# A PEER layer on one core: where the one-token blocks stand in a group, the planner's price of a look-up, skipped empty gather places, and the PSUM tag of the last group's scores

## The chip, the cores and the metric

The kernel runs on one core of a Trainium2 chip. The metric is the device time of one execution in microseconds (us). The executions shown are 1198.37, 1197.64 and 1202.17 us, with a median of 1198.37 us.

## The reference, cut to what matters

One layer of a diffusion backbone: 512 latent tokens and 256 context tokens of width 1024 go through a bidirectional mLSTM, grouped-query attention, a norm, and then PEER, a retrieval of experts. The change lies in PEER. For each block of 128 tokens the reference computes

```python
s1, i1 = lax.top_k(s[:, :, 0], 16);  s2, i2 = lax.top_k(s[:, :, 1], 16)
idx = ...                       # per token 8 heads x 16 experts out of 128 x 128
g = softmax(top_s)
act = gelu(einsum('nd,ned->ne', xt, u[idx]), approximate=False)
out = einsum('ne,ned->nd', g * act, v[idx])
```

Each token picks 128 of 16384 experts; an expert is a row `u` and a row `v` of 1024 floats, kept side by side in one table of rows of 8192 bytes. Many experts are picked by one token of the block only, others by several.

## The kernel before, in words

**Groups and blocks.** The 512 tokens are four groups (NT = 4) of 128. The distinct experts of a group are listed and worked off in 29 blocks (NBL) of 128 places, an expert in each partition. The first 12 lists (NB1) hold experts that one token picked ("one-token blocks"), the other 17 hold the rest ("dense blocks"). The reference's own routing on its inputs gives 3178, 3675, 3632 and 3680 distinct experts in the four groups, with 1405, 1625, 1568 and 1640 of them picked once. 3712 places are there, so 534, 37, 80 and 32 places stay empty. In the first group the empty ones are the lists 26, 27 and 28 (dense) and 11 (one-token) as a whole and a few places more. An empty place has the number 16384 (NEXP). The list `wi` keeps that number, which points at a row of zeros behind the weights; the list `ri` is clipped to 16383, so the expert gather of an empty place fetches the last expert's row.

**A block.** `rows` (stage r, five blocks ahead) gathers the experts' rows `uv` (128 x 8192 bytes, 1.05 MB) and the weights' rows `wr` (128 x 512 bytes) through POOL's queue, line 1122. A dense block is then transposed on PE (`turn`, L1287, copied by ACT, L1288), multiplied with the group's tokens into a PSUM bank `s` (`dense`, L1301), goes through Gelu on ACT (L1302) and is multiplied by the weights on DVE (L1303). A one-token block finds each expert's token on DVE (`token`, L1162 and L1163, four blocks ahead), gathers these tokens' rows `xg` (128 x 4096 bytes, 0.52 MB; `use`, three blocks ahead), takes the products on DVE (`dot`, L1183, one block ahead) and scales on ACT (L1184, L1200). Both end in `add`: `py += wt @ v`, L1211, in PSUM. PIPE gives the stages' lead. `seqs` says which list stands at which of a group's 29 positions; before, the one-token lists stand at positions 3, 5, 7, ... 25 in the first three groups and at 1, 3, 5, 8, 10, 13, 15, 18, 20, 22, 25, 27 in the last.

**Work for the next group.** While one group's blocks run, the next group's lists are made, as a generator that is advanced by a planner: `select` (top-16 on DVE, with scratch in the big tile `work`), then `prelude`. The first part of `prelude`, here "the table", builds the dense weights of 128 x 128 x 128 in `work`: 16 chunks of one-hot tiles A and B on DVE (L1018, L1021), matmuls on PE (L1028, L1031), and ACT copies (L1033). Then 16 pieces of `work` of 512 KB each are written to `Wd` in memory through SP's queue (`rows_out`, L1038), and the lists are looked up (`tables`, `look_up`: DVE, PE L1089, ACT L1095). `select` of the group after that uses `work` again.

**The planner.** Each step of that generator has a price: C_SEL 5 and others for `select` (56 in sum), C_A 3.5 for each of 16 chunks (56), C_L 1.5 for each of 10 look-up steps (15), C_N 1 three times: 130 in sum. After each block as many steps are emitted as 130/29 per block allow, and a piece of `Wd` per step. The frame orders each engine's instructions by this program order and by what is ready.

**PSUM.** In this part the tags are "u" with two banks, "s" with one, "p" with two (the prelude's matmuls), "pf" with one, and `py` with two.

Of the kernel before, what the change touches and what calls it, by code (L numbers as in the profile page):

```python
# [23 lines left out]
NT = L // P  # L24
# [9 lines left out]
NEXP = 16384  # L34
NBL = 29
NB1 = (12, 12, 12, 12)
# [5 lines left out]
EST = (2, 1)  # L42
HLB = 2
WTB = 5
C_SEL, C_OH, C_IIG, C_A, C_L, C_N = 5, 3, 2, 3.5, 1.5, 1
WPC = 16
GH = 4
TCH = 8
# [3 lines left out]
UVB = 7  # L52
# [8 lines left out]
PIPE = (("r", 5), ("k", 4), ("u", 3), ("d", 1), ("o", 2), ("w", 1), ("h", 1), ("a", 0))  # L61
EUV = 3
HEADS = (2, 4, 6, 8, 10, 12, 14, 16, 18, 21, 24, 27, 30, 33, 38, 40)
SPREAD = 0.7
OFF = 0.5
LAG = 2
POL = 1
DMB = 3
# [9 lines left out]
def tile_block(ctx, tc, xcT, x, cb, crow, w_mod1, w_modT, w_in, conv_w, conv_b, b_gates, mhw, qnw, knw,  # L78
# [9 lines left out]
    def bank(name, tag="mm"):  # L88
        t = ps.tile([P, 512], F32, tag=tag, name=name, bufs=depth[tag])
        return t  # L90
# [43 lines left out]
    ident, triu, tril, ones = (cst[:, i, :] for i in range(4))  # L134
# [167 lines left out]
    def g4(name):  # L302
        t = mp.tile([P, 2, 8, 4], F32, name=name)
        return t

    li, lf, e1, b, blast, a, M, amb, m, Ml, winter, enm, wr, decay = (
        g4(n) for n in ("li", "lf", "e1", "b", "blast", "a", "M", "amb", "m", "Ml", "winter", "enm", "wr", "decay"))
# [585 lines left out]
    lists = [None] * NT  # L893
# [90 lines left out]
    def send(n):  # L984

        for _ in range(min(n, len(pieces))):
            f, q = pieces.pop(0)
            f(q)
# [129 lines left out]
        lists[t] = ri, wi  # L1118
        yield

    def gather(dst, src, ids):
        nc.gpsimd.indirect_dma_start(out=dst, out_offset=None, in_=src,  # L1122
                                     in_offset=bass.IndirectOffsetOnAxis(ap=ids, axis=0))


    def order_of(n1, spread):
        def at(b):
            return (b + 0.5) / n1 * spread + (1 - spread) * OFF if b < n1 else (b - n1 + 0.6) / (NBL - n1)
        return sorted(range(NBL), key=at)

    seqs = [order_of(NB1[t], SPREAD if t < NT - 1 else 1.0) for t in range(NT)]

    def blocks(bp, eb):

        n = NBL
# [6 lines left out]
        def rows(t, i):  # L1142
            b = seqs[t][i]
            if i == 0:
                send(WPC)
                hts[t] = channels(t, bp if t % 2 else eb)
            pool, bufs = (eb, EUV) if (t * n + i) % UVB < EUV else (bp, UVB - EUV)
            w = pool.tile([P, 2 * D], F32, tag="uv", name=f"uv{t}_{b}", bufs=bufs)
            gather(w, uv, lists[t][0][:, b:b + 1])
            wr = bp.tile([P, P], F32, tag="wr", name=f"wr{t}_{b}", bufs=LOOK + 2)  # L1150
            gather(wr, Wd[t][:, :], lists[t][1][:, b:b + 1])
            live[t, i] = [w, wr]
# [13 lines left out]
        def use(t, i):  # L1166

            b = seqs[t][i]
            if b < NB1[t]:
                xg = bp.tile([P, D], F32, tag="xg", name=f"xg{t}_{b}", bufs=XGB)  # L1170
                gather(xg, h2d[:, :], live[t, i].pop())
                live[t, i].append(xg)
# [14 lines left out]
        def weights(t, i):  # L1187
            b = seqs[t][i]
            if b >= NB1[t]:
                w, wr, ut = live[t, i]  # L1190
                wt = bp.tile([P, P], F32, tag="wt", name=f"wt{t}_{b}", bufs=WTB)
                dense(t, b, ut, hts[t], wr, wt)
                live[t, i] = w, wt
# [9 lines left out]
        def add(t, i):  # L1203
# [9 lines left out]
            if i == n - 1:  # L1213
# [4 lines left out]
                else:  # L1218
                    ends.append(finish(t, bp, py, lnr))

        stages = {"r": rows, "k": token, "u": use, "d": dot, "o": operand, "w": weights, "h": scaled, "a": add}
        loads = {DEFER - LOOK: 1, AT: 2, n + AT: 3}
        for i in range(-LOOK, len(items)):
            if i + LOOK == len(items):
# [3 lines left out]
                w = bp.tile([P, 2 * D], F32, tag="uv", name="lnr", bufs=UVB - EUV)  # L1228
# [6 lines left out]
            if i in loads:  # L1235

                t = loads[i]
# [53 lines left out]
    def channels(t, pool):  # L1291

        ht = pool.tile([P, KC, P], F32, tag="ht", name=f"ht{t}")
        (nc.gpsimd if t else nc.sync).dma_start(ht, h2Td[t])
        return ht

    def dense(t, b, ut, ht, gr, wt):

        s_ = bank(f"s{t}_{b}", "s")
        for k in range(KC):  # L1300
            nc.tensor.matmul(s_[:, 0:P], ut[:, k, :], ht[:, k, :], start=k == 0, stop=k == KC - 1)  # L1301
        nc.scalar.activation(wt, s_[:, 0:P], AF.Gelu)  # L1302
        nc.vector.tensor_tensor(wt, wt, gr, op=ALU.mult)  # L1303
# [44 lines left out]
    with tc.tile_pool(name="bp", bufs=1, reuse_waits="tile") as bp:  # L1348
        n = NBL
# [22 lines left out]
    with tc.If(most > NBL):  # L1372
        with tc.tile_pool(name="fb", bufs=1) as fb:
            for t in range(NT):
# [8 lines left out]
                with tc.For_i(0, P):  # L1383

                    pm = fb.tile([P, 3, P], F16, tag="fpm", name=f"fpm{t}")
                    nc.vector.tensor_scalar(pm[:, 2], ig[:, 0], bc[:, 0:1], None, op0=ALU.is_equal)
                    for q in range(2):
                        nc.vector.tensor_tensor(pm[:, q], pm[:, 2], ig[:, 2 + q], op=ALU.mult)
                    pl = bank(f"fpl{t}", "p")
                    for c in range(P // TCH):  # L1390
                        A = fb.tile([P, P, TCH], F16, tag="fA", name=f"fA{t}_{c}", bufs=2)
                        nc.vector.tensor_tensor(A, iob, ig[:, 1, c * TCH:(c + 1) * TCH].unsqueeze(1).to_broadcast([P, P, TCH]),
                                                op=ALU.is_equal)
                        for i in range(TCH):
                            j = c * TCH + i
                            for q in range(2):
                                nc.tensor.matmul(pl[:, j:j + 1], A[:, :, i], pm[:, q, j:j + 1], start=q == 0, stop=q == 1)
                    gr = fb.tile([P, P], F32, tag="fgr", name=f"fgr{t}")
                    nc.scalar.mul(gr, pl[:, 0:P], 1.0 / GSC)
                    ri = fb.tile([P, 1], I32, tag="fri", name=f"fri{t}")  # L1400
                    nc.vector.tensor_copy(ri, bc[:, 1:2])
                    w = fb.tile([P, 2 * D], F32, tag="uv", name=f"fw{t}", bufs=2)
                    gather(w, uv, ri)
                    wt = fb.tile([P, P], F32, tag="fwt", name=f"fwt{t}")
                    dense(t, "f", turn(t, "f", fb, w), ht, gr, wt)
                    py = ps.tile([P, D], F32, tag="y", name=f"fpy{t}", bufs=1)
                    for half in range(2):
                        hs = slice(half * 512, half * 512 + 512)
                        nc.tensor.matmul(py[:, hs], wt, w[:, D + half * 512:D + half * 512 + 512], start=True, stop=True)
                    nc.vector.tensor_tensor(y, y, py, op=ALU.add)  # L1410
                    nc.vector.tensor_scalar_add(bc[:, 0:1], bc[:, 0:1], 1.0)
                    nc.vector.tensor_scalar_add(bc[:, 1:2], bc[:, 1:2], float(P))
# [81 lines left out]
```

## Time and profile before

| what | value |
|---|---|
| median of the executions | 1198.37 us |
| profiled execution, its own time | 1204.68 us |
| its span (first to last instruction) | 1202.9 us |
| granted TensorE clock, mean | 0.931 |
| PE, DVE, ACT, POOL busy | 1038.4, 826.4, 464.8, 465.7 us |
| moved by DMA | 284.15 MB, 236 GB/s over the span |

The blocks run from 612 to 1189 us of the span: the four groups' sums `py` are complete near 766, 918, 1076 and 1189 us. In what follows "DMA share" is the mean busy share of the core's 16 DMA engines, and PEclk the granted TensorE clock as a share of full speed.

### The profile page before, as it was taken

What the parts mean: (1) busy time and instruction counts of PE and PEld (TensorE: products, weight loads), DVE (VectorE), ACT (ScalarE), POOL (GpSimd) and SP (SyncE); (2) the same over time, 40 slices, a digit from 0 to 9 for tenths busy, and PEclk for the clock granted to TensorE, in tenths of its full rate; (3) what the DMA queues carried; (4) which work ended last, traced back from release to release, by engine and by line L of the source; (5) the groups of instructions that cost most, each with busy time, mean ns of one, the idle gap of its engine ahead of it and who ended that gap; (6) DMA issues with size and microseconds to landing.
All of it is one profiled execution on the core that took longest, in us unless ns stands there. A gap on an engine that the chain in (4) does not pass through costs nothing.

```text
span 1202.9 us, 19211 instructions
## 1 busy us (share of the span) xinstructions
PE 1038.4 (86%) x6784; PEld 837.7 (70%) x6784; DVE 826.4 (69%) x2698; ACT 464.8 (39%) x1132; POOL 465.7 (39%) x374
## 2 busy tenths in 40 slices
PE   6889689799989999999378987989788797897985
PEld 5688678688988888898346765668555576565663
DVE  5958999869875778377795857989379785223213
ACT  3343353465562121245433454344343353522221
POOL 3643234222023520000345542656335544355760
PEclk7899899989989999999679997999899899898998
DMA  9656450220035498512978889988997877989983
GB/s 364 226 202 217 168 177 36 74 80 15 1 102 173 159 274 252 172 39 108 384 249 305 280 299 371 330 333 286 339 401 282 301 280 285 417 318 340 377 315 115
DMA packets 109038, 284.15 MB, mean 236 GB/s; under 512 B 9316, under 2 KB 62280, under 8 KB 92936
## 3 DMA queue, kind: packets, MB, share of 16 engines
q0 software_dynamic: 28048, 157.04, 35.2%
q1 hardware_dynamic: 75864, 120.32, 29.0%
q10 hardware_dynamic: 5024, 5.51, 1.3%
q8 instruction: 55, 0.90, 0.3%
q14 instruction: 47, 0.39, 0.1%
HBM read 237.17 MB, written 45.66 MB: 235 GB/s over the span
## 4 chain that ended last, share of the span: by engine, by line
PE 38%; DVE 16%; DMA 10%; issue 8%; ACT 2%; SPq 1%; POOL 1%; another core or an unknown queue 0%; DVEq 0%; ACTq 0%; POOLq 0%
PE py L1211 8%; PE pwq L839 8%; PE s L1301 4%; DMA xg<-h2d,ti 4%; PE pW L1031 3%; PE pw L770 2%; PE put L1287 2%; PE po L542 2%; DMA Wd<-work 2%; DVE work L900 2%; DMA uv<-in_uv,ri 2%; DVE work L899 1%; DVE work L902 1%; DVE work L901 1%; PE pf L1028 1%
## 5 line engine op out<-in xcount | busy, mean ns | idle before, releaser
L1211 PE MATMUL py<-uv,wt 128*128 128x512 f32 x464 | 239.7, 636 | 14.6 <-DVE wt L1303 7.8
L1122 POOL DMA_INDIRECT uv<-in_uv,ri x116 | 119.1, 1026 | 133.4 <-PE py L1211 65.0
L1301 PEld LDWEIGHTS s<-ht,ut 128*128 128x128 f32 x1088 | 141.4, 202 | 37.1 <-ACT wt L1302 18.3
L1301 PE MATMUL s<-ht,ut 128*128 128x128 f32 x1088 | 151.5, 289 | 14.8 <-ACT wt L1302 13.9
L1122 POOL DMA_INDIRECT wr<-Wd,wi x116 | 125.6, 1083 | 69.5 <-issue 35.6
L1211 PEld LDWEIGHTS py<-uv,wt 128*128 128x128 f32 x464 | 83.1, 203 | 70.0 <-issue 53.8
L1288 ACT COPY ut<-put 128x512 f32<-128x512 f32 x136 | 75.2, 588 | 102.3 <-PE put L1287 72.1
L1031 PEld LDWEIGHTS <-A 128*128 128x128 f16 x1024 | 89.7, 146 | 20.3 <-issue 13.1
L1033 ACT ACTIVATE work<-pW 128x512 f32<-128x512 f32 x128 | 73.5, 597 | 78.2 <-PE pW L1031 66.5
L1031 PE MATMUL pW<-B,A 128*128 128x128 f16 x1024 | 95.3, 225 | 6.4 <-ACT work L1033 2.9
L1287 PEld LDWEIGHTS put<-cst,uv 128*128 128x128 f32 x544 | 68.3, 152 | 41.8 <-issue 29.9
L1122 POOL DMA_INDIRECT xg<-h2d,ti x48 | 57.9, 1206 | 94.1 <-DVE ti L1163 44.6
L839 PE MATMUL pwq<-h2T,wq 128*128 128x256 f32 x416 | 94.2, 379 | 0.0
L1287 PE MATMUL put<-cst,uv 128*128 128x128 f32 x544 | 80.3, 291 | 15.4 <-DMA uv<-in_uv,ri 13.0
L1183 DVE SCALAR_TENSOR_TENSOR xg<-xg,uv 128x1024 f32<-128x1024 f32 x48 | 58.5, 1219 | 46.5 <-DMA xg<-h2d,ti 46.4
L839 PEld LDWEIGHTS pwq<-h2T,wq 128*128 128x128 f32 x416 | 77.0, 190 | 9.4
L1021 DVE TENSOR_TENSOR B<-B,igr 128x1024 f16<-128x1024 f16 x128 | 82.9, 687 | 1.0
L1018 DVE TENSOR_TENSOR A<-iob,ig 128x1024 f16<-128x1024 f16 x64 | 44.0, 688 | 47.6 <-ACT ig L1004 27.8
L1028 PE MATMUL pf<-B,A 128*128 128x128 f16 x512 | 75.0, 226 | 1.1 <-issue 1.0
L209 POOL TENSOR_TENSOR wlo<-wi,whi 128x1024 fp32r<-128x1024 f32 (+1 forms) x18 | 47.9, 2675 | 60.6 <-ACT whi L208 60.5
L1028 PEld LDWEIGHTS <-A 128*128 128x128 f16 x512 | 60.5, 147 | 8.4 <-issue 6.4
L1303 DVE TENSOR_TENSOR wt<-wt,wr 128x128 f32<-128x128 f32 x68 | 19.6, 289 | 58.1 <-ACT wt L1302 58.1
(437 smaller groups left out, 2315.8 us busy)
## 6 DMA issues: line engine op xcount, KB each, us to landing
Wd<-work SPq DMA_DIRECT2D x64, 512.0 KB
wm<-in_w_modT SPq DMA_DIRECT2D x16, 1024.0 KB
wq<-in_wq SPq DMA_DIRECT2D x26, 512.0 KB
wi<-in_w_in SPq DMA_DIRECT2D x8, 1024.0 KB
wsc<-in_w_mod SPq DMA_DIRECT2D x7, 1024.0 KB
wor<-in_w_out SPq DMA_DIRECT2D x8, 512.0 KB
wql<-in_wq SPq DMA_DIRECT2D x6, 512.0 KB
qkT<-in_w_in SPq DMA_DIRECT2D x2, 1024.0 KB
```

Of the source, the lines that this page charges most:

```text
L209: nc.gpsimd.tensor_tensor(lo[:, k:k + 4, 0:cw], wv[:, k:k + 4], hi[:, k:k + 4, 0:cw].bitcast(F32), op=ALU.subtract)
L839: nc.tensor.matmul(pt, w[:, k, :], h2T[:, k, t0 * P:(t0 + 2) * P], start=k == 0, stop=k == KC - 1)
L1021: nc.vector.tensor_tensor(B[:, q].rearrange("p a n r -> p a (n r)"), (B[:, 0] if q else ior).rearrange("p a n r -> p a (n r)"), igr[:, q, ...
L1028: nc.tensor.matmul(pf[:, 0:P], A[:, :, n], B[:, 0, :, n, :], start=c == 0 and n == 0, stop=c == P // TCH - 1 and n == TCH - 1)
L1031: nc.tensor.matmul(pw[:, (n - n4) * P:(n - n4 + 1) * P], A[:, :, n], B[:, q, :, n, :], start=q == 1, stop=q == 2)
L1033: nc.scalar.mul(Wn[:, :, n0 + n4:n0 + n4 + 4], pw.rearrange("p (n k) -> p k n", n=4), 1.0 / GSC)
L1122: nc.gpsimd.indirect_dma_start(out=dst, out_offset=None, in_=src, in_offset=bass.IndirectOffsetOnAxis(ap=ids, axis=0))
L1183: nc.vector.scalar_tensor_tensor(xg, xg, 1.0, w[:, 0:D], op0=ALU.mult, op1=ALU.mult, accum_out=nf)
L1211: nc.tensor.matmul(py[:, hs], wt, w[:, D + half * 512:D + half * 512 + 512], start=i == 0, stop=i == n - 1)
L1287: nc.tensor.transpose(pt[:, q * P:(q + 1) * P], w[:, (4 * kh + q) * P:(4 * kh + q + 1) * P], ident)
L1288: nc.scalar.copy(ut[:, 4 * kh:4 * kh + 4, :], pt.rearrange("p (q n) -> p q n", q=4))
L1301: nc.tensor.matmul(s_[:, 0:P], ut[:, k, :], ht[:, k, :], start=k == 0, stop=k == KC - 1)
```

## The change: what it does

- `PLACES` takes the place of `SPREAD` and `OFF`: in the first three groups the one-token lists stand at positions 1, 3, 5, 7, 9, 11, 20, 22, 24, 25, 27, 28, so the positions 12 to 19 are dense. In the last group they stand at 1, 3, 6, 8, 10, 13, 15, 18, 20, 22, 25, 27 (one list moves from 5 to 6).
- `C_L` is 3 instead of 1.5: the sum of the prices is 145.
- The gather of `uv` takes its rows by `wi` with a bound of 16383 from the eighth block on, so an empty place is left out and its partition keeps what the buffer held; its weight is zero. The first seven blocks, which fill the seven buffers, still take `ri`.
- In the last group the scores of a dense block go to a bank of tag "p" (two banks) instead of "s" (one).

```diff
-C_SEL, C_OH, C_IIG, C_A, C_L, C_N = 5, 3, 2, 3.5, 1.5, 1
+C_SEL, C_OH, C_IIG, C_A, C_L, C_N = 5, 3, 2, 3.5, 3, 1
...
-SPREAD = 0.7
-OFF = 0.5
+PLACES = (1, 3, 5, 7, 9, 11, 20, 22, 24, 25, 27, 28)
...
-    def gather(dst, src, ids):
+    def gather(dst, src, ids, last=None):
         nc.gpsimd.indirect_dma_start(out=dst, out_offset=None, in_=src,
-                                     in_offset=bass.IndirectOffsetOnAxis(ap=ids, axis=0))
-
-
-    def order_of(n1, spread):
-        def at(b):
-            return (b + 0.5) / n1 * spread + (1 - spread) * OFF if b < n1 else (b - n1 + 0.6) / (NBL - n1)
-        return sorted(range(NBL), key=at)
-
-    seqs = [order_of(NB1[t], SPREAD if t < NT - 1 else 1.0) for t in range(NT)]
+                                     in_offset=bass.IndirectOffsetOnAxis(ap=ids, axis=0),
+                                     bounds_check=last, oob_is_err=last is None)
+
+
+    def order_of(t):
+        n1 = NB1[t]
+        places = PLACES if t < NT - 1 else [int((b + 0.5) / n1 * NBL) for b in range(n1)]
+        ones, more = iter(range(n1)), iter(range(n1, NBL))
+        return [next(ones if i in places else more) for i in range(NBL)]
+
+    seqs = [order_of(t) for t in range(NT)]
...
-            gather(w, uv, lists[t][0][:, b:b + 1])
+
+            if t * n + i < UVB:
+                gather(w, uv, lists[t][0][:, b:b + 1])
+            else:
+                gather(w, uv, lists[t][1][:, b:b + 1], NEXP - 1)
...
-        s_ = bank(f"s{t}_{b}", "s")
+
+        s_ = bank(f"s{t}_{b}", "p" if t == NT - 1 and b != "f" else "s")
```

## Rows read from the trace of the kernel before

**Rows 1.** The page: busy time of the engines, and POOL's DMA queue.

```profile
PE 1038.4 (86%) x6784; PEld 837.7 (70%) x6784; DVE 826.4 (69%) x2698; ACT 464.8 (39%) x1132; POOL 465.7 (39%) x374
...
q0 software_dynamic: 28048, 157.04, 35.2%
```

**Rows 2.** Busy time by stretch: length, engines' busy us, PEclk, DMA share, GB/s.

```profile
704.00:737.00 33.00, 24.63 (x153) 16.61 (x152) 13.28 (x73) 13.88 (x54) 11.35 (x12) 0.89 0.95 361
737.00:790.00 53.00, 47.09 (x243) 33.47 (x243) 51.16 (x267) 20.35 (x56) 28.50 (x25) 0.87 0.88 325
790.00:851.00 61.00, 58.75 (x552) 46.14 (x550) 52.16 (x110) 29.99 (x65) 34.50 (x31) 1.00 0.86 315
851.00:883.00 32.00, 22.82 (x112) 14.85 (x113) 12.97 (x75) 13.34 (x52) 9.92 (x11) 0.84 0.96 375
883.00:946.00 63.00, 49.49 (x285) 34.93 (x285) 53.40 (x270) 22.16 (x62) 36.55 (x32) 0.99 0.89 333
946.00:1004.00 58.00, 56.60 (x515) 44.62 (x515) 49.97 (x104) 29.01 (x60) 28.38 (x26) 0.95 0.73 255
1004.00:1048.00 44.00, 32.40 (x189) 22.09 (x188) 13.62 (x72) 20.92 (x82) 15.61 (x17) 0.84 0.97 383
```

**Rows 3.** SP's queue in order of time: the writes of Wd, start, length, count.

```profile
706.25 27.85 SPq L1038 DMA_DIRECT2D Wd<-work  x16
...
851.91 22.26 SPq L1038 DMA_DIRECT2D Wd<-work  x16
...
1010.96 23.19 SPq L1038 DMA_DIRECT2D Wd<-work  x16
```

**Rows 4.** Waits, 704 to 737 us: us in total, times, longest.

```profile
DVE jt L1162 <- DMA wr<-Wd,wi: 6.2, 1, 6.2
...
DVE work L898 <- DMA Wd<-work: 4.6, 1, 4.6
```

**Rows 5.** Waits, 848 to 895 us.

```profile
DVE xg L1183 <- DMA xg<-h2d,ti: 14.8, 3, 5.5
```

**Rows 6.** Waits, 1004 to 1048 us.

```profile
DVE xg L1183 <- DMA xg<-h2d,ti: 16.6, 3, 6.3
```

**Rows 7.** Timeline at the end of the second table: start, length, instruction, idle before.

```profile
849.45 1.22 DVE L1183 SCALAR_TENSOR_TENSOR xg<-xg,uv 128x1024 f32<-128x1024 f32 x1 [5.51 <-DMA xg<-h2d,ti]
...
850.82 1.06 ACT L1033 ACTIVATE work<-pW 128x512 f32<-128x512 f32 x2
...
879.79 0.47 DVE L898 MAX8 work<-scfx 128x8 f32<-128x128 f32 x2
```

**Rows 8.** The chain that ended last, a dense block in the last group.

```profile
1100.55 0.88 PE put L1287 x8
1101.43 1.79 PE s L1301 x16
1103.21 1.72 PE py L1211 x4
```

**Rows 9.** One line's instructions: ns least, median, longest; first and last start.

```profile
L1122 POOL DMA_INDIRECT uv<-in_uv,ri x116: 932/938/1841, 585.3 to 1170.3; - x116
...
L1183 DVE SCALAR_TENSOR_TENSOR xg<-xg,uv x48: 1169/1220/1284, 621.3 to 1183.2; 128x1024 f32<-128x1024 f32 x48
...
L1162 DVE SCALAR_TENSOR_TENSOR jt<-wr,iof x48: 273/285/318, 609.6 to 1174.3; 128x128 f32<-128x128 f32 x48
...
L1163 DVE TENSOR_SCALAR ti<-tk x48: 131/147/156, 610.0 to 1174.7; 128x1 int32<-128x1 f32 x48
```

**Rows 10.** Busy time by stretch: two stretches with the DMA engines full.

```profile
720.00:740.00 20.00, 13.60 (x66) 8.81 (x67) 10.62 (x66) 7.13 (x31) 2.82 (x3) 0.76 1.01 401
...
1020.00:1048.00 28.00, 22.32 (x115) 14.76 (x114) 7.85 (x48) 17.05 (x72) 9.94 (x11) 0.82 1.02 416
```

**Rows 11.** Busy time by stretch: the last group.

```profile
1076.00:1189.00 113.00, 99.87 (x501) 65.94 (x499) 31.41 (x92) 29.24 (x74) 60.44 (x57) 0.95 0.85 317
```

**Rows 12.** Waits, 1076 to 1189 us: the last group's scores.

```profile
PEld s L1301 <- ACT wt L1302: 5.2, 5, 1.3
```

## The prediction

> **What bounds the kernel now.** First the page: PE is busy for 86% of the span and DVE for 69% [rows 1], so no engine is full on average, and the question is which stage has which limit. The table by stretch shows it [rows 2]. While a table is built (790 to 851 and 946 to 1004 us) PE is busy for 58.8 of 61 us and 56.6 of 58, with DVE close behind (52.2 and 50.0): nothing to gain there. While a selection runs (737 to 790, 883 to 946) DVE is the full one: 51.2 of 53 us and 53.4 of 63. In between lies a stage of 33, 32 and 44 us (704 to 737, 851 to 883, 1004 to 1048) in which PE is busy for only 24.6, 22.8 and 32.4 us, at a granted clock of 0.89, 0.84 and 0.84 (a mean over both levels, 2.4 and 1.2 GHz; it is 1.00 while the second table is built), DVE for 13 us each time, and the DMA engines for 0.95 to 0.97. I call it the copy stage. PE idles there for 8.4 + 9.2 + 11.6 = 29 us; in that and in the clock is what can be won.
>
> What fills the DMA engines there: as soon as a table is complete, its 16 pieces of 512 KB (8.4 MB) go out through SP in one run of 22 to 28 us [rows 3]. The planner sends a piece per step, but the trace shows one burst, so pacing doesn't spread these writes. Full engines move 401 to 416 GB/s [rows 10]: 0.41 MB per us, so the writes alone take 20 us. What makes the engines stand still is latency behind this burst: DVE waits for the token rows `xg` three times in each of the second and third copy stages, 14.8 us and 16.6 us together [rows 5, 6], and in the first once for `wr`, 6.2 us [rows 4]. DVE works in order, so behind a waiting `dot` stand the look-ups and the dense blocks' `wt`, and PE waits for those. One of the waits (5.51 us before 849.45) even lies ahead of the table's last ACT copies (850.82), which the burst itself follows [rows 7].
>
> **What a block needs.** A dense block costs PE 0.88 + 1.79 + 1.72 = 4.39 us [rows 8] and the DMA engines 1.05 + 0.07 = 1.11 MB, 2.7 us at 0.41. A one-token block costs PE 1.72 us, but 1.64 MB or 4.0 us of DMA, and DVE 1.22 + 0.29 + 0.15 = 1.65 us [rows 9]. A dense block pays for its own transfer with PE work, and a one-token block doesn't.
>
> **Order and pacing (one edit, they act together).** With C_L at 3 a group's prices sum to 145. A selection takes 56/145 x 29 = 11.2 blocks (12.5 before), a table 11.2 (12.5), the look-ups with their small steps 33/145 x 29 = 6.6 (18/130 x 29 = 4.0). Lists are due five blocks before the next group, after position 19; counted back, the look-ups fill positions 12.4 to 19 and the table ends at 12.4 instead of 15. Exactly there the change puts eight dense blocks. So the burst meets blocks that have no `xg` gather, whose `uv` rows were asked for five blocks ahead, and whose PE work (4.39 us each) is longer than their transfer. The three waits go: -14.8 us (second group), -16.6 (third), -6.2 at the most in the first.
> Against that: the three `dot`s and `token`s that lay in a copy stage move into the selection, where DVE is full: 3 x 1.65 = +5.0 us per group. Net at best -9.8 and -11.6, and -1.2 in the first. At worst the waits were hidden: the next selection can only start when `work` has been written out (4.6 us of waiting for `Wd` in the first copy stage [rows 4]; the selection after the second burst starts at 879.79, 28 us after the burst began [rows 3, 7]). Then only the wait ahead of the burst (5.5) is gained and 5.0 lost: 0. I take the middle, -5 in the second group and -7 in the third, which has no selection behind it; 0 in the first. What is late next: the selection's DVE, and behind it the gathers of positions 20 to 28, of which six are one-token.
>
> **Empty places.** 683 places are empty; each is a row of 8192 bytes: 5.6 MB of the 157.04 MB of POOL's queue [rows 1]. 534 of them (4.37 MB) are the first group's. Before, list 11 and lists 26 to 28 stand at positions 25 to 28 and are asked for at 20 to 23, in the copy stage; after, they stand at 28 and at 21, 23 and 26, asked for at 16 to 23: still behind the burst. At 401 GB/s [rows 10] that is 10.9 us of full DMA engines. Bounds: 0 (DVE and `work` set the pace) and -10.9; I take -8, since this stretch is the fullest of all. The other 149 places are 1.2 MB or 3 us, in three groups, hidden: 0. What the check costs POOL no row shows. Its gathers take 0.94 us, and the longest 1.84 [rows 9]; between 0 and 0.9 us for each of 109 gathers. POOL is busy for 34.5 of 61 us in its densest table stage [rows 2], so another 0.9 on 13 gathers would still fit: 0, and if one does not fit, it delays a gather that has five blocks of lead.
>
> **Two banks for the last scores.** In the last group PE is busy for 99.9 of 113 us [rows 11]; of its idle time 5.2 us in five waits are for the single bank, until Gelu has read the last block [rows 12]. Bounds 0 and -5.2; a wait saved partly shows up at the next ACT step, so -3. The "p" banks have no other user by then. The list moved from position 5 to 6: 0 (the same work, one block later).
>
> **The sum**, against the profiled execution's own 1204.7 us (span 1202.9, 1.8 around it; it is 6.3 us above the median): -5 - 7 - 8 - 3 = -23, so 1181.7; on the scale of the median, 1198.4 - 23 = 1175, rounded to **1176**. All bounds at their best (-9.8 - 11.6 - 1.2 - 10.9 - 5.2 = -39) give 1160; with returned clock, since the copy stage's 0.84 over 32 and 44 us is worth a few us more, 1157.
>
> **Rivals.**
> 1. *DVE and `work` set the cycle.* From one selection's start to the next lie a selection and a table (53 + 61 us [rows 2]) and the burst (28). If the `xg` waits only filled the burst's time, order and pacing give 0 in the second and third groups and +5 in the first (its three moved blocks' DVE work), and half of the empty places (-4) and of the banks (-1.5) is kept: 1198. For: DVE full in the selections [rows 2]. Against: the third copy stage has no selection behind it and still 16.6 us of waits. Chance 0.11.
> 2. *The burst gets slower.* PE is fed, so gathers go on all the time. If the 16 writes get half of the DMA engines as long as gathers are queued, 8.4 MB need 8.4/0.205 = 41 us and not 28 [rows 3, 7], and two selections start 13 us later: +26 - 23 = 1201. Against: the bursts now end in 22 to 28 us although gathers are queued. Chance 0.08. The Trainium skill, DMA: Bandwidth & Descriptors, Queues, rings and completion order, speaks for it: a DMA engine goes round the queues that have work, a packet from each. The trace doesn't show such an even split: while the second burst ran, 8.4 MB of about 10.5 were the writes.
> 3. *Slower: one-token blocks in a heap.* Positions 20 to 28 hold six of nine, two pairs side by side (24 and 25, 27 and 28). Such a block has 1.72 us of PE work against 4.0 us of DMA; with buffers drained by the burst its `xg` comes late and DVE waits 5.5 us [rows 7], now with a selection queued behind it. Four such waits in all three groups use up the 23 us; two or three in each group (7 x 5.5 = 39) give 1198 + 16 = 1214. For: DMA at 0.88 to 0.89 already in the selections [rows 2]. Against: a selection puts some 4 us of DVE work between two blocks, so that `xg` gets two blocks' time. Chance 0.13.
> 4. *The check doesn't skip*: a place out of bounds is still fetched. The -8 goes: 1184. Chance 0.08, still faster.
>
> **How the numbers follow.** The forecast and its neighbours (1157 to 1188) get 0.60, rival 4 0.08: faster 0.68. Rivals 1 and 2 are within 0.5% (6 us, about what a measurement of this kernel can tell from no change): 0.19. Rival 3: 0.13. The range goes from 1157 (all at best) to 1201 (rivals 1 and 2 in), and leaves out rival 3 and a little below.
>
> **What would show it.** POOL's queue moves 151.4 MB instead of 157.0. In the copy stages the `xg` waits of DVE are gone and PE is busy for over 85%. The three bursts still take 22 to 30 us each, the first group ends some 8 us earlier against its start, and the last group has no wait of the scores' weight load for Gelu. I am wrong if DVE waits long for `Wd` at a selection's start (rivals 1, 2) or for `xg` inside the selections (rival 3).

## The result, and the profile after

The change made the kernel slower: 1205.72 us (median of 12 executions, 1200.08 to 1209.8) against 1198.41 us of the kernel before in the same series. The ratio is 1.0058 with a 95% interval of [1.0035, 1.0082]. The forecast was 1176, the range 1157 to 1201.

The page of the changed kernel, busy times and POOL's queue (the answer to [rows 1]):

```profile
PE 1030.9 (85%) x6784; PEld 831.6 (69%) x6784; DVE 827.7 (69%) x2698; ACT 465.7 (39%) x1132; POOL 478.0 (40%) x374
...
q0 software_dynamic: 28048, 151.44, 34.6%
```

The skipping does what it says: 157.04 - 151.44 = 5.6 MB less, as the 683 empty places foretold. Rival 4 is out. Next the waits of the second copy stage (849 to 885 us) and of the third (1008 to 1045 us) of the changed kernel, the answers to [rows 5, 6]; the columns are us in total, times, longest:

```profile
PE ppr L1066 <- DVE Fw L1063: 6.3, 1, 6.3
...
DVE work L897 <- DMA Wd<-work: 5.9, 1, 5.9
```

```profile
DVE xg L1188 <- DMA xg<-h2d,ti: 9.3, 1, 9.3
...
PE ppr L1066 <- DVE Fw L1063: 6.3, 1, 6.3
```

Where three waits for `xg` stood there is one wait now: in the second stage for the writes of `Wd`, in the third for one `xg`. PE's idle time in these stages only fell from 9.2 of 32 us and 11.6 of 44 [rows 2] to 6.3 of 36 and 6.3 of 37, and these 6.3 us are a single stall each time. The stretches around it, by the view of busy time by stretch:

```profile
866.00:880.00 14.00, 7.68 (x42) 5.97 (x41) 9.15 (x57) 2.12 (x7) 2.89 (x3) 0.76 1.02 418
1025.00:1040.00 15.00, 8.68 (x43) 6.72 (x42) 4.68 (x24) 3.48 (x13) 2.13 (x3) 0.66 1.02 419
```

PE is busy for 7.7 of 14 us and 8.7 of 15, at a clock of 0.76 and 0.66. Over the whole run the `xg` waits weren't saved but moved; first the kernel before, then the changed one, out of all waits of DVE:

```profile
DVE xg L1183 <- DMA xg<-h2d,ti: 46.4, 13, 6.3
```

```profile
DVE xg L1188 <- DMA xg<-h2d,ti: 46.0, 14, 9.3
```

In the last group the wait for the single bank [rows 12] is gone, and another stands in its place: PE's scores now wait for ACT's copies of the transposed rows (1079 to 1193 us):

```profile
PEld s L1307 <- ACT ut L1293: 7.9, 8, 2.2
```

**Where the time went.** The chips of the series differ by up to 2% in this kernel, so both kernels were also profiled on one chip, one execution each (1209.54 and 1212.70 us). First the kernel before, then the changed one, cut at the same events: start of the first table, its burst, start of the second selection, and so on; the last cut is the completion of the third group's sum. Columns as in [rows 2]; the second is the length of the stretch, and the first number in brackets is PE's count of matmuls.

```profile
640.00:706.00 66.00, 61.70 (x569) 48.95 (x568) 52.30 (x111) 31.70 (x67) 35.88 (x32) 1.00 0.79 282
706.00:734.00 28.00, 23.20 (x124) 14.89 (x122) 9.75 (x50) 12.45 (x50) 9.64 (x11) 0.88 1.00 386
734.00:790.00 56.00, 46.38 (x243) 33.12 (x244) 54.20 (x287) 20.77 (x57) 28.91 (x24) 0.91 0.87 319
790.00:852.00 62.00, 59.01 (x555) 46.47 (x554) 52.98 (x114) 30.83 (x66) 35.69 (x33) 1.00 0.86 316
852.00:880.00 28.00, 19.32 (x93) 12.39 (x92) 9.22 (x50) 9.51 (x39) 8.07 (x9) 0.82 0.98 380
880.00:947.00 67.00, 55.33 (x306) 38.82 (x305) 57.20 (x292) 25.93 (x75) 37.26 (x33) 0.96 0.88 331
947.00:1011.00 64.00, 61.07 (x557) 47.72 (x557) 51.84 (x113) 30.28 (x64) 31.04 (x29) 0.96 0.76 268
1011.00:1078.00 67.00, 51.54 (x288) 35.47 (x286) 14.69 (x77) 24.83 (x91) 26.72 (x29) 0.92 0.93 364
```

```profile
635.00:710.00 75.00, 67.57 (x604) 55.65 (x605) 47.55 (x95) 33.06 (x66) 27.88 (x26) 0.93 0.52 177
710.00:731.00 21.00, 17.11 (x110) 11.71 (x109) 9.69 (x54) 9.84 (x40) 8.50 (x9) 1.00 1.00 383
731.00:793.00 62.00, 46.41 (x204) 30.00 (x203) 56.99 (x294) 21.68 (x66) 34.12 (x28) 0.86 0.80 295
793.00:853.00 60.00, 57.26 (x551) 46.28 (x552) 49.94 (x100) 30.22 (x63) 32.71 (x28) 1.00 0.82 300
853.00:873.00 20.00, 19.00 (x131) 14.15 (x129) 4.58 (x28) 10.10 (x38) 6.80 (x7) 1.00 1.01 381
873.00:946.00 73.00, 51.97 (x244) 33.34 (x244) 64.11 (x323) 24.96 (x76) 39.86 (x34) 0.91 0.89 330
946.00:1012.00 66.00, 62.38 (x578) 49.64 (x579) 50.29 (x101) 30.87 (x64) 35.37 (x30) 0.97 0.78 279
1012.00:1083.00 71.00, 59.39 (x332) 41.15 (x331) 20.24 (x95) 27.56 (x100) 34.52 (x34) 0.95 0.98 375
```

The reader is to compare the second column line by line. The stages from a burst to the next selection are shorter, 28 to 21 and 28 to 20 us (-15 together): that is the gain the change was to bring. The selections are longer, 56 to 62 and 67 to 73 (+12). The tables are 66 to 75, 62 to 60 and 64 to 66 us (+9), nearly all of it in the first, where PE has 604 matmuls instead of 569 and the DMA share falls to 0.52. Behind the last burst 67 became 71 (+4), the stretch ahead of the first table (54 to 51) and the last group (116 to 114) give 3 and 2 back: +5 in all.

How the tables share their loss isn't firm. The first two traces, of the kernel before and the changed one on other chips, divide the same +5 otherwise: bursts -14, selections +9, tables +6 (70 and 70, 61 and 65, 64 and 66 us: the first gives nothing), behind the last burst +8, ahead of the first table -4.

### The profile page after: what moved, and what is told of

It reads as the page before. It is cut to its first block, busy times and chain, and to the rows that moved or that the text cites. A ratio compares the mean times of both kernels' runs of the same rounds, so it can differ in the third digit from the quotient of the medians.

```text
span 1207.4 us, 19351 instructions
## 1 busy us (share of the span) xinstructions
PE 1030.9 (85%) x6784; PEld 831.6 (69%) x6784; DVE 827.7 (69%) x2698; ACT 465.7 (39%) x1132; POOL 478.0 (40%) x374
## 3 DMA queue, kind: packets, MB, share of 16 engines
q0 software_dynamic: 28048, 151.44, 34.6%
## 4 chain that ended last, share of the span: by engine, by line
PE 43%; DVE 12%; DMA 8%; issue 6%; ACT 4%; POOL 3%; SPq 1%; another core or an unknown queue 0%; POOLq 0%; DVEq 0%; ACTq 0%
PE py L1216 9%; PE pwq L838 8%; PE s L1307 7%; PE pW L1030 5%; DMA xg<-h2d,ti 4%; PE put L1292 3%; PE pw L769 2%; PE pf L1027 2%; PE po L541 2%; DMA uv<-in_uv,wi 1%; POOL wr L1121 1%; PE ppt L567 1%; ACT Fw L1094 1%; DMA Wd<-work 1%; DVE xg L1188 1%
## 5 line engine op out<-in xcount | busy, mean ns | idle before, releaser
L1216 PE MATMUL py<-uv,wt 128*128 128x512 f32 x464 | 232.7, 629 | 30.4 <-ACT wt L1205 12.4
L1307 PE MATMUL s<-ht,ut 128*128 128x128 f32 x1088 | 155.8, 295 | 27.6 <-ACT wt L1308 13.4
L1121 POOL DMA_INDIRECT uv<-in_uv,wi x109 | 119.4, 1095 | 79.5 <-PE py L1216 47.2
L1030 PEld LDWEIGHTS <-A 128*128 128x128 f16 x1024 | 92.2, 147 | 23.6 <-issue 10.8
L1121 POOL DMA_INDIRECT xg<-h2d,ti x48 | 61.6, 1283 | 75.5 <-DVE ti L1168 34.7
L1292 PE MATMUL put<-cst,uv 128*128 128x128 f32 x544 | 76.2, 281 | 10.8 <-DMA uv<-in_uv,ri 10.4
L1292 PEld LDWEIGHTS put<-cst,uv 128*128 128x128 f32 x544 | 63.7, 146 | 31.0 <-issue 17.9
L1027 PE MATMUL pf<-B,A 128*128 128x128 f16 x512 | 77.8, 225 | 1.8 <-DVE A L1017 1.8
L1027 PEld LDWEIGHTS <-A 128*128 128x128 f16 x512 | 62.3, 147 | 10.1 <-issue 6.0
```

The costliest lines, as they stand in the source:

```text
L1027: nc.tensor.matmul(pf[:, 0:P], A[:, :, n], B[:, 0, :, n, :], start=c == 0 and n == 0, stop=c == P // TCH - 1 and n == TCH - 1)
L1030: nc.tensor.matmul(pw[:, (n - n4) * P:(n - n4 + 1) * P], A[:, :, n], B[:, q, :, n, :], start=q == 1, stop=q == 2)
L1292: nc.tensor.transpose(pt[:, q * P:(q + 1) * P], w[:, (4 * kh + q) * P:(4 * kh + q + 1) * P], ident)
```

## The experiments

All ratios are to the kernel before, timed beside the run on its chip; two versions on different chips are compared by these ratios.

**One part alone, four runs.** *Skipping alone* (the gather by `wi` with a bound from the eighth block on):

> The kernel before with the skipped empty places alone. Prediction: 8 us faster (10.9 at best). Theory O (the order of the blocks is what costs): faster by 2 to 8 us, since the first group's copy stage has 4.4 MB less to move. Theory C (the check costs): POOL's gather with a bound takes 1.00 instead of 0.94 us, 109 times, and POOL's queue is what the blocks wait for: slower by 4 to 7 us.

Measured: 1184.77 us, ratio 0.9870 [0.9831, 0.9910]: 15.6 us faster. Theory C is out, though the check does cost POOL what it said (see the end). The gain is twice what I had taken and above the bound; measured once more (at the end of this section), it was 11 us.

*Banks alone* (`"p" if t == NT - 1 and b != "f" else "s"`):

> The kernel before with the last group's scores in the two p banks alone. Prediction: 3 us faster (5.2 at best). Theory O: 0 to 3 us faster. Rival (the single bank only marks where PE waits for Gelu and the weights anyway): within 1 us.

Measured: 0.9978 [0.9946, 1.0011], 2.6 us faster, which the interval doesn't tell from 0.

*Pace alone* (`C_L` 3):

> The kernel before with C_L = 3 alone. Theory O: the table ends 2.5 blocks earlier, but the copy stage still holds one-token blocks, so the waits for xg stay: within 3 us of before. Rival (the pace alone costs, since the table is squeezed into 11.2 blocks): slower by 5 us or more.

Measured: 0.9991 [0.9964, 1.0018]. No effect by itself.

*Places alone* (the new `order_of` with `PLACES`):

> The kernel before with PLACES alone. Theory O: the table ends late (position 15), so the burst runs into the one-token blocks of positions 20 and 22 and DVE waits for xg there: slower by 5 to 15 us, more than the whole change. Rival (the dense stretch helps by itself): faster by 5 us or more.

Measured: 1231.27 us, 1.0268 [1.0229, 1.0306]: 32 us slower. The order is the part that costs. Its second and third table, by the view of busy time by stretch:

```profile
801.00:869.00 68.00, 65.89 (x619) 53.56 (x617) 48.24 (x95) 32.65 (x67) 29.50 (x29) 1.00 0.70 251
959.00:1030.00 71.00, 69.07 (x636) 55.67 (x636) 50.46 (x101) 34.65 (x71) 33.76 (x32) 1.00 0.76 269
```

PE has 619 and 636 matmuls there instead of 555 and 557, is busy for 97% of the time at full clock, and the DMA share falls to 0.70 and 0.76. The first table (631 to 712 us of this trace) took 81 us with 657 matmuls, against 70 in the first trace of the kernel before. The three are some 24 us longer together, three quarters of the loss. So it is in the main not the wait I had expected (a burst in the one-token blocks): the dense run fell into the table, the one stage in which PE has no room. A dense block has 28 matmuls (8 + 16 + 4, [rows 8]) and a one-token block 4, so 64 and 79 more are about three blocks each. At 4.39 - 1.72 = 2.67 us a block that is an estimate of 7 and 9 us; the two tables are 6 and 7 us longer.

**The change without one part.** First without the order (the old `order_of` is back), then without the pace:

```diff
-PLACES = (1, 3, 5, 7, 9, 11, 20, 22, 24, 25, 27, 28)
+SPREAD = 0.7
+OFF = 0.5
...
-C_SEL, C_OH, C_IIG, C_A, C_L, C_N = 5, 3, 2, 3.5, 3, 1
+C_SEL, C_OH, C_IIG, C_A, C_L, C_N = 5, 3, 2, 3.5, 1.5, 1
```

> The changed kernel with the old order of the blocks (skipping, banks and C_L = 3 kept). If the order is the one part that costs and the rest adds up: before x (0.987 x 0.998 x 0.999), some 18 us faster than before. Rival (the parts work against each other, as the engines' order is made anew each time): within 8 us of before.

Measured: 0.9930 [0.9900, 0.9959], 8 us faster than before. Without the order the change would have been a gain, but of half the size that the single parts promise. So inside the change the order costs some 15 us, and the trace shows where. Its three tables:

```profile
636.00:698.00 62.00, 58.23 (x542) 47.21 (x543) 51.88 (x109) 29.66 (x63) 34.28 (x29) 0.97 0.76 269
776.00:838.00 62.00, 55.52 (x531) 44.18 (x532) 52.20 (x112) 29.78 (x62) 34.12 (x30) 1.00 0.83 296
933.00:993.00 60.00, 57.08 (x548) 46.41 (x547) 51.33 (x109) 30.16 (x63) 35.23 (x29) 0.98 0.84 293
```

They take 184 us together. In the change it is 201 in both of its traces (75 + 60 + 66 above), with 112 matmuls more.

> The changed kernel with C_L = 1.5. If order and pacing act together and the pace repairs part of what the order costs: slower than the change, by 6 us or more (32 - 16 - 3 = 13 us slower than before). If the pace does nothing, as it did alone: equal to the change, 7 us slower than before.

Measured: 1.0217 [1.0170, 1.0263], 26 us slower. So the pace, worth nothing alone, repairs some 19 us of what the order costs; by the planner's prices it moves the table ahead of the dense run.

> The changed kernel without the skipping (all gathers take the clipped list). If the skipping is worth as much here as alone: 13 to 18 us slower than the change, 18 to 25 slower than before; order, pace and banks then cost that much together. If the order had moved the empty lists to where their bytes cost nothing: within 4 us of the change.

Measured (the clipped gather for all blocks): 1.0135 [1.0109, 1.0161]. The skipping is worth 0.8 to 0.9%, 10 us, inside the change; order, pace and banks together cost 16 us.

**Did the skipping gain more than its bytes?** Here the empty places read 128 different rows, not one and the same:

```diff
-        nc.vector.tensor_scalar_min(ri, idf, float(NEXP - 1))
+        nc.vector.tensor_scalar(sp, idf, float(NEXP), pcol1, op0=ALU.is_ge, op1=ALU.mult)
+        nc.vector.tensor_tensor(ri, idf, sp, op=ALU.subtract)
```

> The kernel before, in which the empty places fetch 128 different rows, one per partition, instead of all the same one: all bytes are still moved, with two more small DVE instructions per group. If skipping gains by the bytes left out: within 3 us of before. If it gains because hundreds of reads of one row of memory are slow: faster by 5 us or more.

Measured: 0.9950 [0.9923, 0.9977], 6 us faster with every byte still moved, as expected if many reads of one row are slow. The trace doesn't bear that out. 512 of the 683 empty places are the four lists that the first copy stage gathers, and this stage is as long as before, 28 us at about the same rate (the line to compare is 706.00:734.00 above):

```profile
701.00:729.00 28.00, 22.61 (x124) 14.43 (x122) 9.42 (x50) 12.70 (x50) 9.74 (x11) 0.88 1.00 380
```

With the bytes left out it is 21 us in both runs of the skipping alone, which is about the gain I had forecast for it. Where the 6 us of this run come from isn't shown; its second copy stage happens to be 21 us instead of 28. An edit that adds one small DVE instruction per group has thus moved 6 us, and a difference of that size between two versions can't be put down to one cause by the time alone. The change's own +7 us is hardly larger; the 32, 26 and 15 us that hang on the order are.

**Where the dense run may stand.** Skipping and banks with the pace of before, and the run at positions 20 to 25:

> Skipping and banks, C_L = 1.5, and PLACES = (1, 3, 5, 7, 9, 11, 13, 15, 17, 19, 26, 28): the dense run at positions 20 to 25 instead of 12 to 19. Theory T (the run lies in the table stage, where PE is full and each one-token block replaced by a dense one costs 4.39 - 1.72 = 2.67 us): the table keeps its six one-token blocks, the copy stage loses its xg waits: 18 to 30 us faster than before. Rival D (a dense run costs wherever it stands, since the one-token blocks moved out crowd the selection, where DVE is full): 5 us or more slower than skipping and banks together, so less than 13 us faster than before.

Measured: 0.9906 [0.9870, 0.9941]. Its base, skipping and banks alone:

> Skipping and banks alone, the base for the late run and for the pace. If they add up: 0.987 x 0.998, 18 us faster than before; then the pace costs 10 us on top of them and the late run 7. If the banks are worth nothing beside the skipping: 15 us faster than before.

Measured: 0.9901 [0.9875, 0.9927]. So the late run costs nothing and gains nothing: both theories miss. It keeps the tables nearly as short as before (67, 61 and 60 us), and its copy stages still stop PE: there the next selection waits 13.3 us for `Wd`, with the look-ups queued behind it (waits, 833 to 875 us):

```profile
PE ppk L1088 <- DVE work L971: 12.5, 1, 12.5
```

**Is it the wait for Wd?** The selection's scratch in the first pieces to be written:

```diff
-        sv = scr[:, 7296:7552].rearrange("p (h a) -> p h a", a=16)
+        o = 0 if t else 7296
+        sv = scr[:, o:o + 256].rearrange("p (h a) -> p h a", a=16)
...
```

> The changed kernel with the selection's scratch moved in work (for groups 1 to 3) from the columns of the writes' pieces 7 and 8 to those of pieces 0 and 1, so the next selection can start when the burst's first four pieces have landed, not the first nine. Theory W (the 5.9 us wait for Wd, with the look-ups and all of PE queued behind it, is what is left of the copy stage's stall): the wait goes, 5 to 12 us faster than the change. Rival T (the table stage, full of PE work, costs it all): within 3 us of the change.

Measured: 1.0107 [1.0086, 1.0128], slower than the change. Theory W falls as I put it. The wait went (the selection starts 4 us after the burst began instead of 20), and the chain of this run shows what took its place, in order of time:

```profile
853.13 0.48 DVE work L897 x2
...
865.10 8.54 DMA xg<-h2d,ti
...
875.55 0.14 DVE Fw L1064
875.74 0.29 PE ppr L1067
```

The `xg` of the first one-token block behind the run lands after 8.5 us, and the second list's tables stand behind its `dot` in DVE's order. The third table is longer too, 76 us instead of 66. On skipping and banks the same edit gained nothing either:

> Skipping and banks with the same scratch. Theory W: 5 us or more faster than skipping and banks alone (which waited little for Wd: then less, 0 to 5). Rival T: no difference, within 3 us.

Measured: 0.9925 [0.9899, 0.9951].

**One-token blocks back into the table.** The changed kernel with another order:

```diff
-PLACES = (1, 3, 5, 7, 9, 11, 20, 22, 24, 25, 27, 28)
+PLACES = (1, 3, 5, 6, 8, 9, 11, 12, 21, 23, 25, 27)
```

> The changed kernel with PLACES = (1, 3, 5, 6, 8, 9, 11, 12, 21, 23, 25, 27): the copy stage stays dense from 13 to 20, and the table stage (blocks 4 to 12 in the trace) holds six one-token blocks instead of four, the crowded end of the group four instead of six. Theory T: three tables shorter by 2 x 2.67 us each: 10 to 16 us faster than the change, about 1192. Rival D (DVE, which works on A and B there, takes over as the limit): within 4 us of the change.

Measured: 0.9987 [0.9968, 1.0007], some 8 us faster than the change (between the theories, nearer to T). The second and third tables by stretch:

```profile
776.00:831.00 55.00, 52.19 (x504) 40.93 (x505) 51.36 (x104) 27.36 (x61) 37.70 (x29) 1.00 0.86 312
919.00:981.00 62.00, 57.63 (x540) 45.36 (x539) 53.62 (x120) 28.43 (x62) 37.13 (x33) 1.00 0.90 331
```

504 and 540 matmuls instead of 551 and 578, and 55 and 62 us instead of 60 and 66, with DVE nearly as busy as PE (51.4 of 55 us). Part of it came back as a longer wait for `Wd` (10.0 us instead of 5.9).

**The run up to position 22**, the first 13 positions as in the run before this one (`PLACES = (1, 3, 5, 6, 8, 9, 11, 12, 23, 25, 26, 28)`), beside the change again and the kernel before:

> The changed kernel with PLACES = (1, 3, 5, 6, 8, 9, 11, 12, 23, 25, 26, 28): the first 13 positions hold eight one-token blocks as in the run before it, and the dense run goes on to position 22. Theory X (what stops PE in the copy stage is the first one-token block behind the run: its xg, asked for inside the burst, lands 8.5 us later, and the second list's tables stand behind its dot in DVE's order): the third group's stall of 14 us goes, the second's is left to the wait for Wd; 8 us or more faster than the run with ones in the table, so 16 us faster than the change. Rival (the burst stalls whatever stands first behind it): within 4 us of that run.

> The changed kernel itself beside these, on the same chip: 1.006 of before again (1.003 to 1.010). If the change's loss hangs on the chip it ran on: below 1.002 or above 1.012.

> The kernel before, for a trace on the same chip: table stages of 60 to 65 us, burst to the next selection 28 us, the last group 107 to 112 us.

Measured: 0.9915 [0.9888, 0.9942] for the longer run, 1.0049 [1.0023, 1.0076] for the change. On one chip 16 us lie between them, which is theory X's number, but its mechanism isn't what the trace shows. The change's loss is no matter of the chip. The single execution of the kernel before took 1209.5 us; its tables were 62 to 66 us and its bursts 28 us, the last group 116. In the third copy stage of the longer run the wait for the first `xg` behind the run is not gone. It is longer than in the change (9.4 us):

```profile
1030.96 1.23 DVE L1188 SCALAR_TENSOR_TENSOR xg<-xg,uv 128x1024 f32<-128x1024 f32 x1 [10.65 <-DMA xg<-h2d,ti]
```

PE's longest stall there is 5.2 us instead of 6.4. Cut by stretch as above, the longer run gains in the stretch ahead of the first table (6 us), in the tables (9) and in the selections (8); its first two copy stages are 2 us longer together, and the stretch behind the last burst 4. The 9 us go with the one-token blocks that were put back; what shortened the others isn't shown.

> The same with the selection's scratch in the first pieces. Theory X with W (two waits in a row, of which either alone hides the other's removal): faster than the run before it by 3 to 8 us, and no PE stall of over 6 us in any copy stage. Rival: no faster, as the scratch alone gained nothing.

Measured: 0.9935 [0.9907, 0.9962]. No faster than the longer run, though its wait for `Wd` is down from 10.0 to 1.3 us. What stops DVE in its place was not taken apart.

**The version that beats both.** Skipping alone, once more:

> The kernel before with the skipping alone, on the same chip: 0.987 of before again (0.983 to 0.991), which makes it the fastest of all the versions here, or as fast as skipping with banks (0.990).

Measured: 0.9910 [0.9878, 0.9942]; 0.9870 the first time. Skipping alone, skipping with banks (0.9901) and the longer run (0.9915) can't be told apart; the simplest is to keep the old order and the old pace.

## Why the prediction was wrong

**The step that failed first: "nothing to gain there".** I read from [rows 2] that PE is full while a table is built and then left the stage out of the sum. Full means that it can lose. The order takes one-token blocks out of positions 13 to 19, and where these are replaced by dense ones within the table stage each costs PE 2.67 us. I had placed the table at positions 1.2 to 12.4, which by the same arithmetic holds for the second and third groups only. In the first, the next group's work has 18 blocks instead of 29 (START and LATE in the kernel), so the table lies at positions 8 to 15, in the dense run; PE has 35 matmuls more there. What the stage costs is shown by the order: alone it makes the three tables some 24 us longer, inside the change 17 us longer than without it, and the one-token blocks put back make them shorter again. Against the kernel before the change's tables are only 6 to 9 us longer, since the pace by itself shortens them (60, 61 and 60 us in its run). That the matmul count of the stage goes with its length is shown; how many us each moved block costs is an estimate from [rows 8].

**The step that failed next: "the three waits go" (-5 and -7).** The next selection did start 7 and 8 us sooner. In the first copy stage, though, the skipping alone does as much (28 to 21 us in both of its runs). And the third group, of which I took -7, lost: behind its burst 67 us became 71. I had also counted one wait too many there: [rows 2] cut the third table at 1004 us, 7 us before its burst [rows 3], so the first of the three waits of [rows 6] lies in the table. The three waits were not removed but gathered into one that is worse placed. The widened look-ups put the second list's tables late in the burst, behind the selection's first instruction and behind the `dot` of position 20, whose `xg` is asked for three blocks ahead, inside the burst. The engines' order in the changed kernel, in the second and third copy stages of the trace on the one chip (start, length, instruction, idle before):

```profile
867.79 0.94 POOL L1121 DMA_INDIRECT xg<-h2d,ti  x1 [0.30 <-issue]
873.08 0.49 DVE L897 MAX8 work<-scfx 128x8 f32<-128x128 f32 x2 [5.81 <-DMA Wd<-work]
876.27 1.22 DVE L1188 SCALAR_TENSOR_TENSOR xg<-xg,uv 128x1024 f32<-128x1024 f32 x1
877.90 0.22 DVE L1063 COPY Fw<-pft 128x128 f16<-128x128 f16 x1
878.18 0.29 PE L1066 MATMUL ppr<-trinb,Fw 128*128 128x128 f16 x1 [6.18 <-DVE Fw L1063]
...
1027.14 0.94 POOL L1121 DMA_INDIRECT xg<-h2d,ti  x1 [0.30 <-issue]
1035.76 1.22 DVE L1188 SCALAR_TENSOR_TENSOR xg<-xg,uv 128x1024 f32<-128x1024 f32 x1 [9.42 <-DMA xg<-h2d,ti]
1037.11 0.22 DVE L1063 COPY Fw<-pft 128x128 f16<-128x128 f16 x1
1037.39 0.29 PE L1066 MATMUL ppr<-trinb,Fw 128*128 128x128 f16 x1 [6.43 <-DVE Fw L1063]
```

PE, in order itself, holds all dense blocks behind that one small matmul. Moving position 20 out to 23 didn't remove the wait for `xg` (10.65 us there), and removing the wait for `Wd` alone gained nothing; what would empty this stage was not found.

**The selections (+5.0 per group): right.** 3 x 1.65 us of DVE were to move into a stage that DVE fills; the two selections hold 6 and 7 `dot`s instead of 3 each, and measured +6 and +6 us on one chip, +4 and +6 between the first two traces.

**Empty places (-8):** right in kind, somewhat small. Alone -16 and -11, in the change -10; in the first copy stage, where the -8 were expected, it is -7 in both runs of the skipping alone. What the first run gained beyond that isn't explained. The check's price on POOL, costed at 0, wasn't measured by itself.

**Banks (-3):** -2.6, not told from 0; in the changed kernel the wait went and one for the copies took its place. (The sum of the parts gives 1175, which I put down as 1176; nothing hangs on it.)

**The rivals.** Rival 1 (0.11) named the wait for `Wd` and rival 3 (0.13) the one-token block behind the burst whose `xg` comes late; both are seen, the one in the second copy stage and the other in the third, and neither has the tables. Rival 2 is out: fed dense blocks, the bursts end sooner, not later. I had written that the trace speaks against what the Trainium skill says (DMA: Bandwidth & Descriptors, Queues, rings and completion order), that the DMA engines go round the queues that have work. It doesn't: 28 us is the time until the next selection can start, which doesn't need all 16 pieces, and not the time of the writes. In these 28 us (851.9 to 879.8) of the kernel before, q1, which carries the writes, and q0, POOL's queue, moved half each (packets, MB, share):

```profile
q1 hardware_dynamic: 1461, 5.35, 50.3%
q0 software_dynamic: 902, 5.26, 47.2%
```

The even split of the bytes that I priced as a rival was there already. In the changed kernel, with fewer gathers beside the burst, q1 moved 4.78 of 7.69 MB in the 20 us up to the selection.

## What to carry to other kernels

When work is moved within an overlapped schedule, list for every stage which engine is full, and cost what moves *into* a full stage as carefully as what leaves the starved one; do it for the first round as well, where the stages lie elsewhere. A stall behind an in-order engine is not removed by taking away the waits one sees: ask which waiting instruction would stand at the same place next, and what is queued behind it. Parts that look like one package are worth measuring alone: here a 1% gain lay beside a 2.7% loss.

## What the runs showed of the hardware that was not expected

Reads of one and the same 8 KB row by four whole lists (512 places) were no slower than reads of 128 different rows. POOL's queue in 25 us of the first copy stage, first the kernel before (713 to 738 us), then the run with 128 rows (708 to 733):

```profile
q0 software_dynamic: 974, 5.44, 56.6%
```

```profile
q0 software_dynamic: 980, 5.47, 57.2%
```

A place that a gather leaves out still counts as a packet, but a small one: the number of packets of POOL's queue stays at 28048, and those under 512 B grow by 685, which is the 683 places and two more. First the page of the kernel before, then that of the changed one:

```profile
DMA packets 109038, 284.15 MB, mean 236 GB/s; under 512 B 9316, under 2 KB 62280, under 8 KB 92936
```

```profile
DMA packets 109040, 278.56 MB, mean 231 GB/s; under 512 B 10001, under 2 KB 62965, under 8 KB 93621
```

And a gather with a bound takes POOL longer, 1002 ns in the median against 942 for the seven without one in the same run and 938 for the 116 of the kernel before [rows 9], with a register move of 29 ns before each (one line's instructions, least, median, longest):

```profile
L1121 POOLq MOVE  x109: 29/29/35, 606.0 to 1172.6; - x109
L1121 POOL DMA_INDIRECT uv<-in_uv,wi x109: 987/1002/2284, 612.8 to 1174.0; - x109
...
L1121 POOL DMA_INDIRECT uv<-in_uv,ri x7: 937/942/1005, 585.3 to 609.6; - x7
```
